# Attention on one core: TensorE's order written out, products with V in one run two tiles late, and half of a convolution's products on ScalarE

## The chip, the core and the metric

The kernel runs on one core of one Trainium2 chip. A core has five engines that run at the same time and wait for each other through semaphores: TensorE (PE in the profile; PEld is its weight loads), VectorE (DVE), ScalarE (ACT), GpSimd (POOL) and SyncE (SP), whose queue issues most DMAs. TensorE writes to PSUM, and the kernel divides the PSUM into banks of three groups: five called A, two called T, one called V. Everything else is in SBUF. The metric is the time of one execution on the device in microseconds (us); lower is better.

## The reference, cut to what matters

One step of a small diffusion transformer: two layers, 128 context tokens and 1024 latent tokens, 1024 channels, fp32. In each layer three mixers read the same normalised input, and their outputs are concatenated and projected:

```python
def layer(x, cond, lp, rope=None, ctx=None):
    mod = (silu(cond) @ lp['w_ada'] + lp['b_ada'])        # six vectors of 1024: shift, scale, gate, twice
    h = rmsnorm(x, lp['g_mix']) * (1 + sc1) + sh1
    comb = h @ lp['w_in']
    attn = mla_mixer(...)      # 8 heads; k is 64 + 32 rotary wide, v is 64 wide
    ssm = ssd_mixer(...)       # a state-space scan
    conv = conv_module(...)
    x = x + g1 * (concat([attn, ssm, conv]) @ lp['w_out'])
    ...                        # then a SwiGLU feed-forward, gated in the same way

def block_attention(q, k, v):  # for each block of 128 queries
    s = einsum('bqhd,bkhd->bhqk', qi, k) * scale
    p = softmax(s)
    return einsum('bhqk,bkhd->bqhd', p, v)

def conv_module(comb, lp):     # 256 channels
    g = comb[..., :256] * sigmoid(comb[..., 256:])
    g = dwconv(g, cm_conv_w, cm_conv_b)       # 31 taps along the tokens, per channel
    return silu(layernorm(g, cm_ln_g, cm_ln_b))
```

The context's queries see only the context's keys. The latent tokens' queries see 128 cached keys and the 1024 latent keys (1152).

## The kernel before, in words

**Layers and stages.** For each layer l the kernel projects the input (w_in), runs the scan, prepares the latents of attention, runs the attention loop, projects with w_out, and runs the feed-forward. The tokens are held as columns in three chunks of 384. Products that must keep fp32 accuracy are three matmuls on high and low parts (mm3, lines 103 to 105).

**The attention loop.** Eight heads are taken in four pairs i (prep_k and prep_q make a pair's keys and queries, prep_v and prep_r those of two pairs), and the 1152 queries in nine tiles t of 128 queries: 36 tiles in a layer. For one tile, `scores(j)` makes the scores of head j in three blocks of 384 keys (nine matmuls into three A banks), the maximum of each block on VectorE (line 805), their maximum and its negative (807, 808), and three exps on ScalarE (810), with the sums beside them. `attend` turns the probabilities: 18 transposes (831) of 128x128 into T banks, four at a time, copied to `pt` by VectorE (836) or ScalarE (84), and after each group of four the products with V (842) that belong to it, into the V bank. Two matmuls spread the reciprocal sums over the rows (853; ScalarE copies them to `rs`), and a product makes the output `mo` (856). Tile t = 0 is the context's, with one block of 128 keys. `attend` of a tile runs between the scores of the next one.

**Beside the tiles.** In layer 0 only, 80 steps of `adas` (186: eight small matmuls each, which make the modulation vectors of later stages) are drawn in between. In both layers `conv_taps` makes the convolution on GpSimd: for each half j of the 256 channels an initial product (869) and 30 taps, each a product into `ct` (872) and an addition into `acc` (78), over 1167 columns. A `copy` at 865 is its first instruction and holds it back to the start of the loop. `conv_norm` makes the layer norm of a chunk in four pieces: sums over channels on TensorE (882), centring (886), squares (890, 892, 78), sums of squares on TensorE (897), a reciprocal square root of ten small VectorE instructions (145 to 151), and a spread of it on TensorE (160), after which 905 and 906 finish.

**What sets the order.** The program is traced by a tile framework that inserts the semaphores and, by a simulated timeline, puts each engine's instructions into an order of its own: program order is a priority there, not the order on an engine. Each engine then executes its list in order. Pools with a fixed number of buffers (`bufs`) add waits: an exp's bank is free only when the exp has been read, a tile in SBUF only when its last reader is done. After the loop, line 971 loads the first w_out weights with load_w: ScalarE makes a high part `wh` (84), GpSimd the low part `wl` (81), 1024 columns each.

Of the kernel before, what the change touches and what calls it, by code (L numbers as in the profile page):

```python
# [8 lines left out]
F32 = mybir.dt.float32  # L9
# [8 lines left out]
KD = 8  # L18
# [35 lines left out]
def build(tc, nc, ap, dbg=None):  # L54
    V, S, G, PE, Q = nc.vector, nc.scalar, nc.gpsimd, nc.tensor, nc.sync
# [110 lines left out]
    def adas(rounds, stage=None, ahead=2):  # L166

        stage = stage or wp
        steps = [(l, r, q, k) for l, r in rounds for q in range(4) for k in range(0, KD, 2)]
        loads = []  # L170
        m = None
        for n in range(len(steps) + ahead):
            if n < len(steps):
                l, r, q, k = steps[n]
                loads.append(stage.tile([128, 1024], F32, tag="ws", name="ws", bufs=ahead + 1))
                Q.dma_start(loads[-1], ap["w_ada"][l, r, q, k // 2])
            if n >= ahead:
                l, r, q, k = steps[n - ahead]
                st = loads.pop(0)
                if k == 0:  # L180
                    m = sm.tile([128, 128], F32, tag="ms", name="ms", bufs=2)
                b = bank("A")
                for kk in range(2):
                    for j in range(4):
                        o = 512 * kk + 128 * j
                        PE.matmul(b[32 * j:32 * j + 32, :128], cond[:, k + kk, :], st[:, o:o + 128],
                                  start=kk == 0, stop=kk == 1)
                if k:
                    add_to(V, m, b[:, :128], m)
                else:  # L190
                    copy(m, b[:, :128])
                if k == KD - 2:
                    ada_end(l, r, q, m)
            yield
# [99 lines left out]
    first = adas([(0, 0)], sp, 6)  # L294
# [15 lines left out]
    for l in range(L):  # L310
# [397 lines left out]
        def prep_v(r, cs=range(NC3)):  # L708
            if r:
                vt[r] = hl_tile("vv", F32)[:, :2560].rearrange("p (t n) -> p t n", t=10)  # L710
            w = lat["w"][0]
            for c in cs:
                ck = lat[c][1]
                for t in range(KC[c][0] // 128, KC[c][1] // 128):
                    b0 = bank("A")
                    o = 128 * t - KC[c][0]
                    mm3(b0[:, :256], [(ck[:, 0, o:o + 128], ck[:, 1, o:o + 128],
                                       w[0][:, 512 + 256 * r:768 + 256 * r], w[1][:, 512 + 256 * r:768 + 256 * r])])
                    copy(vt[r][:, t], b0[:, :256])

        def prep_k(i, cs=range(NC3)):
            w = lat["w"][0]
            for c in cs:
                a, b = KC[c]
                b0 = bank("A")
# [18 lines left out]
        def prep_r(r, cs=range(NC3)):  # L744
            if r not in qr:
                qr[r] = at.tile([128, T], F32, tag="qr", name="qr", bufs=1)
            for c in cs:
                tb = [at.tile([128, CH], F32, tag="tb", name="tb", bufs=4) for _ in range(2)]
                for n in range(2):
                    Q.dma_start(tb[n], ap["rf"][:, c, n])  # L750
                    b0 = bank("A")
                    o = 512 * n + 128 * r
                    mm3(b0[:, :CH], [(wr[0][:, o + 256 * k:o + 256 * k + 128], wr[1][:, o + 256 * k:o + 256 * k + 128],
                                      lat[c][0][:, 0, k], lat[c][0][:, 1, k]) for k in range(2)])
                    V.tensor_mul(tb[n], tb[n], b0[:, :CH])
                add_to(V, qr[r][:, CH * c:CH * c + CH], tb[0], tb[1])
# [4 lines left out]
        prep_r(0, (0, 1))  # L761
        prep_k(0, (2,))
        prep_v(0, (2,))
        prep_r(0, (2,))
# [19 lines left out]
        class Tile_:  # L784


            def __init__(self, i, t, q, mo):
                self.i, self.t, self.q, self.mo = i, t, q, mo
                self.sl = small(8, "sl", 3)
                self.prs = []  # L790

            def scores(self, j):
# [3 lines left out]
                blocks = [(0, 128)] if t == 0 else [(128 + CH * b, CH) for b in range(3)]  # L796
                n = len(blocks)
                pr = at.tile([128, T], F32, tag="P", name="P", bufs=4)
                mx = small(4, "mx", 3)
                bs = []  # L800
                for b, (k0, w) in enumerate(blocks):
# [4 lines left out]
                if n > 1:  # L806
                    V.reduce_max(mx[:, 3:4], mx[:, 0:3], axis=AX.X)
                V.tensor_scalar_mul(mx[:, 3:4], mx[:, 3:4] if n > 1 else mx[:, 0:1], -SCALE)  # L808
                for b, (k0, w) in enumerate(blocks):
                    S.activation(pr[:, CH * b:CH * b + w], bs[b][:, :w], AF.Exp, bias=mx[:, 3:4], scale=SCALE,  # L810
                                 accum_out=sl[:, 3 * j + b:3 * j + b + 1])
                self.prs.append(pr)
                if j == 1:
# [4 lines left out]
                    else:  # L818
                        V.reciprocal(sl[:, 6:8], lv[:, :, 0])

            def attend(self):
                i, t, prs, sl, mo = self.i, self.t, self.prs, self.sl, self.mo
                vv = vt[i // 2]
                kts = [0] if t == 0 else list(range(1, 10))
                ob = bank("V")
                for a in range(0, len(kts), 2):
                    grp = kts[a:a + 2]
                    tb = bank("T")
                    for u in range(len(grp)):
                        for j in range(2):  # L830
                            PE.transpose(tb[:, 256 * u + 128 * j:256 * u + 128 * j + 128],  # L831
                                         prs[j][:, 128 * (a + u):128 * (a + u) + 128], ident)
                    pt = at.tile([128, 512], F32, tag="pt", name="pt", bufs=3)
                    w = 256 * len(grp)
                    if a % 4:
                        V.tensor_copy(pt[:, :w], tb[:, :w])  # L836
                    else:
                        copy(pt[:, :w], tb[:, :w])
                    for u, kt in enumerate(grp):
                        for j in range(2):  # L840
                            h = 2 * (i % 2) + j
                            PE.matmul(ob[64 * j:64 * j + 64, :128], vv[:, kt, 64 * h:64 * h + 64],  # L842
                                      pt[:, 256 * u + 128 * j:256 * u + 128 * j + 128],
                                      start=kt == kts[0], stop=kt == kts[-1])
                    if a == 4:
                        yield

                dl = at.tile([128, 2, 128], F32, tag="dl", name="dl", bufs=2)
                V.tensor_tensor(dl, ident.unsqueeze(1).to_broadcast([128, 2, 128]),
                                sl[:, 6:8].unsqueeze(2).to_broadcast([128, 2, 128]), ALU.mult)  # L850
                rb = bank("T")
# [3 lines left out]
                copy(rs, rb[:, :128])  # L855
# [4 lines left out]
        acc = [None, None]  # L860

        def conv_taps():
# [3 lines left out]
            for j in range(2):  # L866
# [45 lines left out]
        prev = iter(())  # L912
        qs = {}
        for i in range(NPAIR):
            if i:
                prep_k(i)
            if i == 2:
                prep_r(1)
            qs[i, 0] = prep_q(i, 0)
            for c in range(NC3):  # L920
                mo = at.tile([128, CH], F32, tag="mo", name="mo", bufs=2)
                for t in range(3 * c, 3 * c + 3):
                    cur = Tile_(i, t, qs[i, c], mo)
                    cur.scores(0)
                    if i == 2 and t == 1:
                        prep_v(1)
                    next(ag, None)
                    next(prev, None)
                    cur.scores(1)
                    next(ag, None)  # L930
                    drain(prev)
                    prev = cur.attend()
                    if t == 3 * c and c + 1 < NC3:
                        qs[i, c + 1] = prep_q(i, c + 1)
                    if t % 2:
                        next(ag, None)
# [4 lines left out]
        drain(prev)  # L941
        drain(norms)
        at.release()
# [27 lines left out]
        wo = [load_w(ap["w_out"][l, m]) for m in range(4)]  # L971
# [210 lines left out]
```

## Time and profile before

| | us |
|---|---|
| median of three runs (lowest, highest) | 3270.39 (3269.64, 3280.65) |
| the profiled execution, and its span | 3282.06, 3280.3 |
| PE busy in the span | 3120.5 (95%) |
| VectorE, ScalarE, GpSimd busy | 1754.9, 1144.7, 1070.2 |
| mean granted clock of TensorE | 0.976 |
| attention loop of layer 0, from line 865 to the last `mo` | 310.8 to 730.0 |
| attention loop of layer 1, from line 865 to the last `mo` | 1938.2 to 2314.1 |

A matmul is pipelined, and its recorded end is a model: a matmul of 384 columns is recorded with 0.34 us, though the next one starts 0.17 us later, so PE is not at its peak where it reads as busy. The granted clock is 1.0 at TensorE's full rate (2.4 GHz) and 0.5 at its lower one (1.2 GHz). A ScalarE exp is recorded with 0.58 us, and the next one starts 0.56 us after it.

### The profile page before, as it was taken

The numbers are of one execution on the slowest core, as the hardware profiler recorded it, in microseconds if no ns is written. First come the engines' busy times: TensorE is split into PE (matmuls) and PEld (weight loads), VectorE is DVE, ScalarE is ACT, GpSimd is POOL, SyncE is SP. The second block draws the span as 40 slices with busy tenths as digits, with TensorE's granted clock in tenths as the row PEclk, the third lists the DMA queues.
The fourth block names the chain that finished last, engine by engine and source line by source line (L and its number), as shares of the span: only waits on it lengthen the run. The fifth ranks groups of instructions, "written<-read, shape, count | busy, mean of one in ns | idle before, by whom it ended". The sixth has DMA issues, their size and how long they took to land. (4 is left out here: it accounts for less than half of the span.)

```text
span 3280.3 us, 50736 instructions
## 1 busy us (share of the span) xinstructions
PE 3120.5 (95%) x20610; PEld 2899.1 (88%) x20610; DVE 1754.9 (53%) x3891; ACT 1144.7 (35%) x2677; POOL 1070.2 (33%) x601
## 2 busy tenths in 40 slices
PE   6997998999999999999999989987999999999997
PEld 5986767779999999999999867766999999999997
DVE  6768777663633333333386687765373333333335
ACT  4465544562411111111144656555341111111113
POOL 2302998012511211112142049871242121122112
PEclk9998999999999999999999989998999999999998
DMA  6112333342111111111121020000401111111111
GB/s 236 49 30 86 115 117 105 123 173 76 52 39 39 45 46 39 39 39 52 47 95 55 25 64 8 20 15 22 149 27 51 40 46 46 39 39 52 39 33 58
DMA packets 67004, 202.38 MB, mean 62 GB/s; under 512 B 7889, under 2 KB 25425, under 8 KB 65233
## 3 DMA queue, kind: packets, MB, share of 16 engines
q1 hardware_dynamic: 63456, 194.02, 17.9%
q10 hardware_dynamic: 3312, 5.11, 0.4%
q8 instruction: 162, 2.65, 0.3%
q14 instruction: 74, 0.60, 0.1%
HBM read 177.44 MB, written 21.66 MB: 61 GB/s over the span
## 5 line engine op out<-in xcount | busy, mean ns | idle before, releaser
L81 POOL TENSOR_TENSOR wl<-ws,wh 128x1024 fp32r<-128x1024 f32 x164 | 396.0, 2421 | 1629.3 <-ACT wh L84 1549.3
L103 PE MATMUL psA<-hh,wh 128*128 128x384 f32 x2496 | 836.5, 337 | 4.4 <-ACT hh L270 2.7
L104 PE MATMUL psA<-hl,wh 128*128 128x384 f32 x2496 | 837.7, 336 | 1.1 <-DVE hl L267 0.7
L105 PE MATMUL psA<-hh,wl 128*128 128x384 f32 x2496 | 837.3, 336 | 0.0
L103 PEld LDWEIGHTS psA<-hh,wh 128*128 128x128 f32 x2496 | 471.0, 189 | 8.1 <-ACT hh L270 3.7
L104 PEld LDWEIGHTS psA<-hl,wh 128*128 128x128 f32 x2496 | 471.1, 189 | 3.9 <-DVE hl L267 1.2
L105 PEld LDWEIGHTS psA<-hh,wl 128*128 128x128 f32 x2496 | 471.0, 189 | 0.6
L999 DVE TENSOR_TENSOR fs<-fs,psA 128x384 f32<-128x384 f32 x132 | 72.9, 553 | 666.3 <-PE psA L105 657.4
L78 POOL TENSOR_TENSOR acc<-ct,acc 128x1167 f32<-128x1167 f32 x120 | 325.9, 2716 | 9.9
L84 ACT ACTIVATE wh<-ws 128x1024 fp32r<-128x1024 f32 (+1 forms) x178 | 184.8, 1049 | 405.2 <-PE psA L104 197.9
L998 ACT ACTIVATE fs<-psA 128x384 f32<-128x384 f32 x132 | 63.9, 485 | 655.1 <-PE psA L105 655.1
L810 ACT ACTIVATE P<-psA,mx 128x384 f32<-128x384 f32 (+1 forms) x400 | 224.1, 571 | 126.2 <-DVE mx L808 88.2
L1052 DVE SCALAR_TENSOR_TENSOR x<-psT,mod,x 128x384 f32<-128x384 f32 (+1 forms) x320 | 157.7, 513 | 198.6 <-PE psT L105 198.6
L805 DVE TENSOR_REDUCE mx<-psA 128x1 f32<-128x384 f32 (+1 forms) x400 | 208.9, 539 | 77.5 <-PE psA L105 74.9
L1052 DVE SCALAR_TENSOR_TENSOR x<-psA,mod,x 128x384 f32<-128x384 f32 (+2 forms) x384 | 186.7, 512 | 53.4 <-PE psA L105 46.9
L1002 DVE TENSOR_TENSOR fl<-fs,fh 128x384 fp32r<-128x384 f32 x132 | 167.5, 1270 | 65.9 <-ACT fh L84 65.9
L842 PE MATMUL psV<-pt,vv 128*64 128x128 f32 x2336 | 195.2, 289 | 6.7 <-DVE pt L836 5.0
L831 PE MATMUL psT<-cst,P 128*128 128x128 f32 x1168 | 194.5, 288 | 3.0 <-ACT P L810 1.1
L104 PE MATMUL psA<-fl,wh 128*128 128x384 f32 x576 | 193.2, 336 | 0.0
L105 PE MATMUL psA<-fh,wl 128*128 128x384 f32 x576 | 193.2, 335 | 0.0
L103 PE MATMUL psA<-fh,wh 128*128 128x384 f32 x576 | 190.0, 337 | 2.7 <-DVE fs L999 2.7
L103 PE MATMUL psA<-K,q 128*128 128x384 f32 (+1 forms) x400 | 159.1, 398 | 28.7 <-ACT P L810 22.5
(265 smaller groups left out, 5865.3 us busy)
## 6 DMA issues: line engine op xcount, KB each, us to landing
ws<-w_ada SPq DMA_DIRECT2D x96, 512.0 KB, 3.3
ws<-w_gate SPq DMA_DIRECT2D x44, 512.0 KB, 3.7
ws<-w_up SPq DMA_DIRECT2D x44, 512.0 KB, 3.6
ws<-w_down SPq DMA_DIRECT2D x44, 512.0 KB, 3.6
x<-xT SPq DMA_DIRECT2D x6, 1536.0 KB, 7.6
ws<-w_fm SPq DMA_DIRECT2D x16, 512.0 KB, 3.4
ws<-w_out SPq DMA_DIRECT2D x16, 512.0 KB, 3.7
mf<-mixed SPq DMA_DIRECT2D x18, 384.0 KB, 5.6
```

The source lines that it names most:

```text
L78: eng.tensor_tensor(out, a, b, ALU.add)
L81: eng.tensor_tensor(out, x, hi.bitcast(F32), ALU.subtract)
L84: S.activation(out, x, AF.Copy)
L103: PE.matmul(out, sh, mh, start=i == 0, stop=False)
L104: PE.matmul(out, sh, ml, start=False, stop=False)
L105: PE.matmul(out, sl, mh, start=False, stop=i == n - 1)
L805: V.reduce_max(mx[:, b:b + 1], b0[:, :w], axis=AX.X)
L810: S.activation(pr[:, CH * b:CH * b + w], bs[b][:, :w], AF.Exp, bias=mx[:, 3:4], scale=SCALE, accum_out=sl[:, 3 * j + b:3 * j + b + 1])
L831: PE.transpose(tb[:, 256 * u + 128 * j:256 * u + 128 * j + 128], prs[j][:, 128 * (a + u):128 * (a + u) + 128], ident)
L842: PE.matmul(ob[64 * j:64 * j + 64, :128], vv[:, kt, 64 * h:64 * h + 64], pt[:, 256 * u + 128 * j:256 * u + 128 * j + 128], start=kt == kts ...
L1002: V.tensor_sub(fl[:, sl], sg, fh[:, sl].bitcast(F32))
L1052: V.scalar_tensor_tensor(X[c][:, m, a:b], b0[:, a:b], modT[l][:, 40 + m, s:s + 1], X[c][:, m, a:b], ALU.mult, ALU.add)
```

## The change

**TensorE's order.** A small class stands in for the tensor engine. While the attention loop is traced, each matmul and transpose is made to depend on the one before it (without a semaphore), so that TensorE's list is the order of the program. The loop is written in the order that TensorE is to have. For one tile: the three blocks of scores of head 0; all 18 products with V of the tile two back and the two matmuls that spread its sums; two or three `adas` steps in layer 0; the first eight transposes of the tile before; two blocks of scores of head 1; eight transposes; the third block; the last two transposes; and behind them the queries of a next chunk, pieces of prep_r, three taps and, from tile 30 on, two pieces of the norm. `pt` becomes one buffer for a whole tile, `P` has three buffers for four, `mo` three for two, the spread sums go to free columns of the V bank, and `dl` (the diagonal of the reciprocals) is made in `scores`.

**The convolution.** For the half j = 0 the taps are unchanged. For j = 1 ScalarE makes each tap's product in two halves of 583 and 584 columns (`S.activation` with Copy and the tap's weight as scale), and GpSimd only adds, also in halves. Both halves of the channels use one `ct`.

**Smaller edits.** The w_out weights are loaded behind the last tap (`issue_after`). prep_v copies two tiles of V at a time; prep_k and prep_r take their banks before their first matmul; `adas` orders its loads differently and makes the same matmuls.

```diff
-    V, S, G, PE, Q = nc.vector, nc.scalar, nc.gpsimd, nc.tensor, nc.sync
+    V, S, G, Q = nc.vector, nc.scalar, nc.gpsimd, nc.sync
+    pin = {"on": False, "last": None}
+    def pinned(i):
+        if pin["on"]:
+            if pin["last"] is not None:
+                tc.add_manual_dep(i.ins, pin["last"], mybir.DependencyInfo(
+                    mybir.DependencyClass.NoSync, mybir.DependencyReason.DATA), reason="pinned")
+            pin["last"] = i.ins.name
+        return i
...
+            def turn(self):
+                self.pt = at.tile([128, 2, T], F32, tag="pt", name="pt", bufs=1)
+                todo = [(j, u) for u in range(len(self.kts)) for j in range(2)]
...
+                    tb = bank("T")
+                    for n, (j, u) in enumerate(part):
+                        PE.transpose(tb[:, 128 * n:128 * n + 128], self.pr[j][:, 128 * u:128 * u + 128], ident)
...
             def attend(self):
-                    tb = bank("T")
...
+                for u, kt in enumerate(self.kts):
+                    for j in range(2):
+                        h = 2 * (i % 2) + j
+                        PE.matmul(ob[64 * j:64 * j + 64, :128], vv[:, kt, 64 * h:64 * h + 64],
+                                  self.pt[:, j, 128 * u:128 * u + 128], start=u == 0, stop=u == n - 1)
                 for j in range(2):
-                    PE.matmul(rb[64 * j:64 * j + 64, :128], ones[:, 0:64], dl[:, j], start=True, stop=True)
+                    PE.matmul(ob[64 * j:64 * j + 64, 256:384], ones[:, 0:64], self.dl[:, j], start=True, stop=True)
...
                 for t in range(1, 31):
-                    G.tensor_scalar(ct[:, :CO], glu[j][:, t:t + CO], P("cw", w0 + t), 1.0, ALU.mult, ALU.mult)
-                    add_to(G, acc[j][:, :CO], ct[:, :CO], acc[j][:, :CO])
+                    for a, b in ((0, CO // 2), (CO // 2, CO)) if j else ((0, CO),):
+                        if j:
+                            S.activation(ct[:, a:b], glu[j][:, t + a:t + b], AF.Copy, scale=P("cw", w0 + t))
+                        else:
+                            G.tensor_scalar(ct[:, a:b], glu[j][:, t + a:t + b], P("cw", w0 + t), 1.0, ALU.mult, ALU.mult)
+                        last_tap[0] = G.tensor_tensor(acc[j][:, a:b], ct[:, a:b], acc[j][:, a:b], ALU.add)
                     yield
...
                     cur = Tile_(i, t, qs[i, c], mo)
-                    cur.scores(0)
+                    s0, s1 = cur.scores(0), cur.scores(1)
+                    if t:
+                        drain(s0)
+                    if pend:
+                        pend.attend()
                     if i == 2 and t == 1:
                         prep_v(1)
-                    next(ag, None)
-                    next(prev, None)
-                    cur.scores(1)
-                    next(ag, None)
-                    drain(prev)
-                    prev = cur.attend()
+                    step(ag, 2 + (t % 4 == 1))
+                    step(turn, 2)
+                    drain(s0)
+                    step(s1, 2)
+                    step(turn, 2)
+                    drain(s1)
+                    drain(turn)
+                    pend, prev, turn = prev, cur, cur.turn()
...
-                    for _ in range(3):
-                        next(taps, None)
-                    if 9 * i + t >= 25:
-                        next(norms, None)
+                    step(taps, 3)
+                    if 9 * i + t >= 30:
+                        step(norms, 2)
...
-        wo = [load_w(ap["w_out"][l, m]) for m in range(4)]
+        with tc.issue_after(last_tap[0].ins):
+            wo = [load_w(ap["w_out"][l, m]) for m in range(4)]
```

What the change does to the engines' lists is shown at three places of layer 1; the tiles' names carry numbers where two of a kind differ.

TensorE before, in pair 0: most of one tile and the start of the next (K and q make scores, psT holds transposes, psV the products with V).

```order
L842 MATMUL psV<-pt,vv 64x128 x8
L831 MATMUL psT<-cst,P 128x128 x6
L103 MATMUL psA<-K_18407,q_18713 128x384
L104 MATMUL psA<-K_18407,q_18713 128x384
L105 MATMUL psA<-K_18407,q_18713 128x384
...
L842 MATMUL psV<-pt,vv 64x128 x4
L831 MATMUL psT<-cst,P 128x128 x2
L842 MATMUL psV<-pt,vv 64x128 x4
L853 MATMUL psT<-dl,ones 64x128 x2
L842 MATMUL psV<-pt,vv 64x128 x2
L831 MATMUL psT<-cst,P 128x128
```

And TensorE after, in the same pair, one whole tile; the wrapper's two lines, 70 and 74, now stand for every matmul and transpose of the loop.

```order
L70 MATMUL psA<-K_18284,q_18618 128x384 x9
L70 MATMUL psV<-pt,vv 64x128 x18
L70 MATMUL psV<-dl,ones 64x128 x2
L74 MATMUL psT<-cst,P 128x128 x8
L70 MATMUL psA<-K_18285,q_18623 128x384 x6
L74 MATMUL psT<-cst,P 128x128 x8
L70 MATMUL psA<-K_18285,q_18623 128x384 x3
L74 MATMUL psT<-cst,P 128x128 x2
```

The kinds of work no longer alternate in groups of one to eight: a tile is seven groups, the same ones in every tile.

ScalarE before, in pair 1, from the 77th to the 85th exp of the loop.

```order
L810 ACTIVATE P,sl<-psA,mx 128x384 x3
L84 ACTIVATE pt<-psT 128x512 x2
L810 ACTIVATE P,sl<-psA,mx 128x384 x3
L84 ACTIVATE pt<-psT 128x256
L84 ACTIVATE rs<-psT 128x128
L810 ACTIVATE P,sl<-psA,mx 128x384 x3
```

And ScalarE after, from the 77th exp on, where the first products of the convolution (ct) stand.

```order
L104 ACTIVATE rs<-psV 128x128
L104 ACTIVATE pt<-psT 128x2x2x128
L912 ACTIVATE ct<-glu_17227,par 128x583
L912 ACTIVATE ct<-glu_17227,par 128x584
L104 ACTIVATE pt<-psT 128x2x2x128
L104 ACTIVATE pt<-psT 128x2x128
L912 ACTIVATE ct<-glu_17227,par 128x583
L847 ACTIVATE P,sl<-psA,mx 128x384 x3
L912 ACTIVATE ct<-glu_17227,par 128x584
L912 ACTIVATE ct<-glu_17227,par 128x583
```

From here 60 products stand among the exps and copies of 7.5 tiles; the first of them stands ahead of the 80th exp in ScalarE's list.

GpSimd before, late in the taps of the half j = 1: a low part of the w_out weights stands between a tap's product and its addition.

```order
L872 TENSOR_SCALAR ct<-glu_17349,par 128x1167
L81 TENSOR_TENSOR wl<-ws,wh 128x1024
L78 TENSOR_TENSOR acc_19856<-ct,acc_19856 128x1167
L872 TENSOR_SCALAR ct<-glu_17349,par 128x1167
```

And GpSimd after, where the half j = 0 ends and the half j = 1 begins.

```order
L914 TENSOR_SCALAR ct<-glu_16798,par 128x1167
L915 TENSOR_TENSOR acc_18630<-ct,acc_18630 128x1167
L915 TENSOR_TENSOR acc_19678<-ct,acc_19678 128x583
L915 TENSOR_TENSOR acc_19678<-ct,acc_19678 128x584
```

GpSimd has no product left in the half j = 1, and the four `wl` stand behind the last tap.

## Rows read from the trace of the kernel before

**Rows 1.** Windows, each loop in three; us, busy (instructions) per engine, clock, DMA.

```profile
310.80:446.30 135.50, 122.72 (x1253) 92.02 (x1254) 104.88 (x236) 68.42 (x205) 129.78 (x67) 0.96 0.35 117
446.30:564.30 118.00, 109.22 (x1090) 84.16 (x1089) 86.58 (x192) 58.59 (x176) 112.91 (x57) 0.97 0.32 108
564.30:730.00 165.70, 161.69 (x1656) 122.49 (x1654) 111.49 (x331) 101.58 (x274) 11.47 (x5) 1.00 0.42 143
1938.20:2062.30 124.10, 114.48 (x950) 93.70 (x951) 96.23 (x239) 78.85 (x231) 118.89 (x61) 0.99 0.03 11
2062.30:2170.50 108.20, 99.14 (x795) 83.36 (x794) 78.18 (x180) 63.24 (x184) 91.43 (x46) 0.94 0.05 15
2170.50:2314.20 143.70, 116.66 (x954) 91.08 (x952) 86.68 (x248) 83.18 (x219) 41.70 (x21) 0.89 0.14 47
```

**Rows 2.** Timeline of ScalarE, four exps; start us, us, engine, line, tiles.

```profile
446.33 0.59 ACT L810 ACTIVATE P<-psA,mx 128x384 f32<-128x384 f32 x1
564.32 0.59 ACT L810 ACTIVATE P<-psA,mx 128x384 f32<-128x384 f32 x1
2062.32 0.58 ACT L810 ACTIVATE P<-psA,mx 128x384 f32<-128x384 f32 x1
2170.47 0.59 ACT L810 ACTIVATE P<-psA,mx 128x384 f32<-128x384 f32 x1
```

**Rows 3.** Waits of the weight loads, layer 0; us, times, longest us.

```profile
PEld psV L842 <- issue: 17.8, 80, 0.4
PEld psT L831 <- issue: 17.7, 100, 0.3
PEld psA L186 <- issue: 10.3, 51, 0.4
```

**Rows 4.** The same, layer 1.

```profile
PEld psV L842 <- issue: 16.2, 77, 0.4
PEld psT L831 <- issue: 15.5, 86, 0.3
```

**Rows 5.** GpSimd's groups by shape, layer 1's loop; count, busy us, mean ns, idle.

```profile
L78 POOL TENSOR_TENSOR acc<-ct,acc 128x1167 f32<-128x1167 f32 x60 | 162.6, 2711 | 4.9
L872 POOL TENSOR_SCALAR ct<-glu,par 128x1167 f32<-128x1167 f32 x60 | 79.2, 1320 | 5.7
L869 POOL TENSOR_SCALAR acc<-glu,par 128x1167 f32<-128x1167 f32 x2 | 2.9, 1478 | 0.0
```

**Rows 6.** Timeline of GpSimd, layer 1, a `wl` among the taps; idle in brackets.

```profile
2193.66 2.37 POOL L81 TENSOR_TENSOR wl<-ws,wh 128x1024 fp32r<-128x1024 f32 x1 [16.88 <-PE psA L105]
```

**Rows 7.** GpSimd's groups by shape, whole span: other lengths.

```profile
L447 POOL TENSOR_TENSOR of<-xst,wd 128x512 f32<-128x512 f32 x18 | 20.9, 1164 | 101.8 <-ACT xst L84 101.8
L81 POOL TENSOR_TENSOR wlw_zb<-ws,whw_zb 128x792 fp32r<-128x792 f32 x2 | 4.3, 2158 | 4.8 <-ACT whw_zb L84 4.8
```

**Rows 8.** ScalarE's groups by shape, whole span.

```profile
L779 ACT ACTIVATE q<-qr,cst 64x384 fp32r<-64x384 f32 x48 | 29.5, 614 | 14.0 <-DVE qr L78 7.1 <-PE psA L105 5.9
L84 ACT ACTIVATE mh<-mf 128x384 fp32r<-128x384 f32 x48 | 20.7, 510 | 3.0 <-DMA mf<-mixed 1.6 <-DVE mo L856 1.5
L84 ACT ACTIVATE wh<-ws 128x832 fp32r<-128x832 f32 x8 | 7.2, 894 | 10.7 <-PE psA L104 6.5 <-issue 4.2
```

**Rows 9.** Waits of TensorE's matmuls, layer 1's loop.

```profile
PE psA L882 <- POOL acc L78: 19.7, 1, 19.7
PE psA L103 <- ACT P L810: 17.0, 14, 3.1
PE psT L897 <- DVE lsq L78: 2.6, 1, 2.6
```

**Rows 10.** Window behind the longest of these waits, columns as in Rows 1.

```profile
2228.30:2240.10 11.80, 9.15 (x33) 6.53 (x34) 5.20 (x20) 3.48 (x6) 0.00 (x0) 0.50 0.01 1
```

**Rows 11.** Timeline of VectorE, the first norm of layer 1: ends of its chain.

```profile
2234.90 0.16 DVE L899 TENSOR_SCALAR nv<-psT 128x3 f32<-128x3 f32 x1 [1.60 <-PE psT L897]
2237.50 0.56 DVE L157 TENSOR_TENSOR dg<-cst,ry 128x384 f32<-128x384 f32 x1
```

More of the change, by code (lines that the diff above doesn't have):

```diff
@@ L164, in build, with adas @@
     KO = (0, 4, 1, 5, 2, 6, 3, 7)
-    def adas(rounds, stage=None, ahead=2):
-        stage = stage or wp
-        steps = [(l, r, q, k) for l, r in rounds for q in range(4) for k in range(0, KD, 2)]
+    def adas(rounds, stage=None, ahead=2, per=1):
+        steps = [(l, r, q, k) for l, r in rounds for q in range(4) for k in range(0, KD, 2 * per)]
         loads = []
         m = None
[L172 to L193, printed above, removed]
@@ new lines, in load @@
+        def load(l, r, q, k):
+            bufs = 3 if stage is None else ahead + 1
+            sts = [(stage or wp).tile([128, 1024], F32, tag="ws", name="ws", bufs=bufs) for _ in range(per)]
+            for i, st in enumerate(sts):
+                Q.dma_start(st, ap["w_ada"][l, r, q, k // 2 + i])
+            loads.append(sts)
+        for s in steps[:ahead]:
+            load(*s)
+            if stage is not None:
+                yield
+        for n, (l, r, q, k) in enumerate(steps):
+            if stage is not None and n + ahead < len(steps):
+                load(*steps[n + ahead])
+            sts = loads.pop(0)
+            if k == 0:
+                m = sm.tile([128, 128], F32, tag="ms", name="ms", bufs=2)
+            b = bank("A")
+            for kk in range(2 * per):
+                for j in range(4):
+                    o = 512 * (kk % 2) + 128 * j
+                    PE.matmul(b[32 * j:32 * j + 32, :128], cond[:, k + kk, :], sts[kk // 2][:, o:o + 128],
+                              start=kk == 0, stop=kk == 2 * per - 1)
+            if k:
+                add_to(V, m, b[:, :128], m)
+            else:
+                copy(m, b[:, :128])
+            if stage is None and n + ahead < len(steps):
+                load(*steps[n + ahead])
+            if k == KD - 2 * per:
+                ada_end(l, r, q, m)
@@ L293, in build @@
     sp = pool("sp")
-    first = adas([(0, 0)], sp, 6)
+    first = adas([(0, 0)], sp, 6, 1)
     for _ in range(4):
@@ L742, in build, with prep_r @@
         qr = {}
-        def prep_r(r, cs=range(NC3)):
+        def prep_r(r, c):
             if r not in qr:
                 qr[r] = at.tile([128, T], F32, tag="qr", name="qr", bufs=1)
[L747 to L756, printed above, removed]
+            tb = [at.tile([128, CH], F32, tag="tb", name="tb", bufs=4) for _ in range(2)]
+            for n, b0 in enumerate([bank("A") for _ in range(2)]):
+                Q.dma_start(tb[n], ap["rf"][:, c, n])
+                o = 512 * n + 128 * r
+                mm3(b0[:, :CH], [(wr[0][:, o + 256 * k:o + 256 * k + 128], wr[1][:, o + 256 * k:o + 256 * k + 128],
+                                  lat[c][0][:, 0, k], lat[c][0][:, 1, k]) for k in range(2)])
+                V.tensor_mul(tb[n], tb[n], b0[:, :CH])
+            add_to(V, qr[r][:, CH * c:CH * c + CH], tb[0], tb[1])
         drain(so)
@@ L760, in build @@
         at = pool("at")
-        prep_r(0, (0, 1))
+        prep_r(0, 0)
+        prep_r(0, 1)
         prep_k(0, (2,))
         prep_v(0, (2,))
-        prep_r(0, (2,))
+        prep_r(0, 2)
         def prep_q(i, c):
@@ L788, in __init__ @@
                 self.i, self.t, self.q, self.mo = i, t, q, mo
+                self.blocks = [(0, 128)] if t == 0 else [(128 + CH * b, CH) for b in range(3)]
+                self.kts = [0] if t == 0 else list(range(1, 10))
                 self.sl = small(8, "sl", 3)
-                self.prs = []
+                self.pr = []
             def scores(self, j):
@@ L821, in attend @@
             def attend(self):
-                i, t, prs, sl, mo = self.i, self.t, self.prs, self.sl, self.mo
+                i, t, mo = self.i, self.t, self.mo
                 vv = vt[i // 2]
-                kts = [0] if t == 0 else list(range(1, 10))
                 ob = bank("V")
-                for a in range(0, len(kts), 2):
-                    grp = kts[a:a + 2]
-                    tb = bank("T")
[L829 to L851, printed above, removed]
+                n = len(self.kts)
+                for u, kt in enumerate(self.kts):
[3 more added lines that the diff above has]
+                                  self.pt[:, j, 128 * u:128 * u + 128], start=u == 0, stop=u == n - 1)
@@ L911, in build @@
         norms = chain_(*(conv_norm(c) for c in range(NC3)))
-        prev = iter(())
+        pend, prev, turn = None, None, iter(())
         qs = {}
+        pin.update(on=True, last=None)
+        qs[0, 0] = prep_q(0, 0)
         for i in range(NPAIR):
```

88 lines of the change are left out of this document (59 added, 29 removed).

## The prediction

> **What bounds the kernel now.** I read the two attention loops only, since everything outside them keeps its instructions. First the windows [rows 1]: each loop is cut in three where the new list of ScalarE has its first and its last product of the convolution. Counted in the lists, these stand behind the 67th and the 120th of 200 exps in layer 0 and behind the 79th and the 135th in layer 1; the starts of these exps in the trace [rows 2] are the borders. I call the parts A, B and C. The reader is to see that PE is busy for 122.7 of 135.5 us, 109.2 of 118.0 and 161.7 of 165.7 in layer 0, and for 114.5 of 124.1, 99.1 of 108.2 and 116.7 of 143.7 in layer 1, while ScalarE is busy for about half of A and B. PE is the bound, apart from the last part of layer 1. GpSimd is nearly as full in A and B: the convolution occupies it without a break.
>
> Second the waits of the weight loads for "issue" [rows 3, 4]: PE loses time where the kind of its work changes. The three large ones add to 45.8 us in layer 0, the two of layer 1 to 31.7. In the trace I counted 552 changes of kind (scores and preparations, transposes, products with V, adas) in layer 0 (175, 142 and 235 in A, B and C) and 445 in layer 1 (159, 124, 162), so one costs 0.083 and 0.071 us.
>
> Third PE's own waits in layer 1 [rows 9]: 19.7 us for the last addition of the convolution, then 2.6 for a sum of squares, and behind them 11.8 us at a granted clock of 0.50 [rows 10], half of which, 5.9 us, is lost. The convolution is late there because two `wl` of w_out stand among its taps; the later waited 16.9 us with GpSimd idle [rows 6]. In all 28 us of layer 1's C come from this.
>
> **The change part by part.** *TensorE's order.* The new list changes kind about 7 times in a tile and 8 with adas. For C's 14.4 tiles that is 115 in layer 0 for 235 and 105 in layer 1 for 162: 120 x 0.083 = 10 us and 57 x 0.071 = 4 us saved. The same in A (77 and 59 fewer) brings PE's work from 122.7 to 116 us and from 114.5 to 110; in B (82 and 71 fewer) from 109.2 to 102 and from 99.1 to 94. The matmuls are the same ones. A fixed order also takes from PE the freedom to fill a wait: in two of three norms in each layer the three small sums of squares and the spread that needs their square root now stand side by side. VectorE's chain between them runs from 2234.90 to 2238.06, 3.2 us [rows 11]; before, transposes and products of another tile lay beside it. Two in each layer cost 6.4 us.
>
> *The half j = 0 and part A.* Its taps are unchanged on GpSimd: two initial products of 1.48 us and 30 x (1.320 + 2.711 + 0.18 of gaps) = 126.3, in all 129.3 us from line 865 on [rows 5]. There is one `ct`, so ScalarE's first product for j = 1 must wait for the last of these additions, and behind it in ScalarE's list stand the copies of `pt` and the 68th or 80th exp, which PE needs. PE would be there after 116 and 110 us. So A ends at 129.3 in both layers: 6 us less than 135.5, and 5 more than 124.1. PE is held for 13 and 19 us. A stall of 19.7 us was followed by 5.9 us lost to the clock [rows 9, 10]; it could be nothing to 5.9 each time, and I take 2.5, 5 in all.
>
> *The half j = 1 and part B.* A product on ScalarE of 583 or 584 columns isn't in the trace. The nearest row is the same operation, Copy with a pointer as scale, at 384 columns: 614 ns; copies without it took 510 ns at 384 columns and 894 at 832, so 0.857 ns a column [rows 8]. 614 + 200 x 0.857 = 785 ns; bounds are 614 below and 894 above. Sixty make 47 us, added to the 58.6 and 63.2 us that ScalarE is busy with in the same exps now [rows 1]: 106 and 110 us. GpSimd's halves, half of 2.711 and a gap of 0.09, are 1.45 us each (between 1.16 for 512 columns and 2.16 for 792 [rows 7]), 87 us in all: beside it. PE's 102 and 94 us are also below ScalarE's. With 4% of idle between ScalarE's waits I take 110 and 115 us: 8 less than 118.0, 7 more than 108.2.
>
> By the Trainium skill ("ScalarE: Activation LUTs", section "What ACT_TABLE_LOAD costs") an ACTIVATE takes 186 ns and 0.833 ns a column, 93 more for a pointer, and 93 less back to back: an estimate of 765 ns, or 672 where the products follow one another. The 384-column row, 614 where the page gives 599, agrees. By it the sum would be 2 to 13 us lower.
>
> *Part C.* Layer 0: 10 saved, 6.4 lost, -3. Layer 1: the convolution ends at 129.3 + 115 = 244 us after line 865, before the first norm asks, so 22.3 us of waits and 5.9 of clock go; 4 are saved and 6.4 lost: -26. What is late next there is PE itself.
>
> *Edits at no cost.* The w_out weights' four `wl` behind the last tap take about 10 us of an idle GpSimd, some 100 us before w_out needs them; had w_out to wait, it would cost at most these 10. V's copies by two tiles, the other buffers, and adas' loads lie beside PE. A bank waited for by head 1's third block would show as before under "ACT P" [rows 9], 17 us in layer 1; I leave that size as it is.
>
> *Sum.* Layer 0: -6 - 8 - 3 = -17. Layer 1: +5 + 7 - 26 = -14. Clock +5. In all -26 us. The profiled execution took 3282.06 us (span 3280.3), so 3256 on its basis; it lies 11.7 above the median, 3270.39, and the median would become **3244**.
>
> **The rivals.** *More is saved.* Products at 614 ns (-20 in both layers, GpSimd's 87 us then still below), no clock lost (-5) and the norms' chains hidden because ScalarE and the other engines run ahead (-13): -64, 3206. For it speaks that PE's work in A and B is well below the floors; against it that 200 more columns must cost something. Chance 0.20.
>
> *No change that can be told.* ScalarE's list alternates products that wait for GpSimd with exps that wait for PE. If each waits in turn and B has 15% of idle rather than 4%, B is 12 us longer in both layers: -2, 3268. For it: the sum rests on one stall removed, and each part of layer 1 before it becomes longer. Against it: GpSimd has over 20 us to spare in B. Chance 0.24.
>
> *Slower.* The place is B. ScalarE's list is in order; a product that is not ready holds the exps, PE runs dry and its clock falls, as behind the 19.7 us [rows 9, 10]. If PE has the clock at 0.5 for half of B, its 102 and 94 us become 153 and 141: +43 and +26 over what I took, in all +43, 3313. It decides from the point where more than about 36% of B is at 0.5: then the gain of 26 is gone and the loss is over 16. For it: ScalarE is full in B, and PE idles for 8 and 21 us there by my sum. Against it: in A of layer 0 PE had 12.8 us idle and kept a clock of 0.96 [rows 1]. Chance 0.14. The Trainium skill ("TensorE: Matmul & The Clock Gate", Part 1) calls ScalarE's queue strictly first in, first out; nothing in the trace of before speaks against it, and this rival is what that rule would do here at its worst.
>
> That the change does not do what it says is excluded by the lists: PE's order is the written one.
>
> **How the numbers follow.** The forecast has 0.42, with its own range of 3228 to 3262. 0.5% is 16.4 us, about what a measurement can tell from no change: faster is below 3254, slower above 3287. Of the forecast's 0.42 some 0.31 lie below 3254. With 0.20 of the first rival and a little of the second that gives 0.53 for faster; 0.11 and 0.19 make 0.30 for the same; 0.14 and the second rival's tail make 0.17 for slower. The range goes from the first rival, 3204, to 3290, and leaves out most of the slower rival and the far end of the first.
>
> **What would show it.** In the profile after: the first product of ScalarE starts 129 us after GpSimd's first copy in both layers, with PE idle before it; a product lasts 0.78 us and a half addition 1.45; from the first to the last product 110 and 115 us, with ScalarE over 90% busy; the convolution's wait of 19.7 us is gone, and two waits of some 3 us stand at the norms in each layer; waits for "issue" fall by a third. Wrong would be: products shorter than 0.65 us, PE not held at the end of A, or a clock near 0.5 in a long stretch of B.

## The result: 1.3% slower, and the profile after

The changed kernel took 3316.85 us (median of four, 3311.05 to 3324.22) where the kernel before took 3275.52 beside it: a ratio of 1.0128, 95% interval 1.0105 to 1.0151, +41 us. The forecast was 3244. The profiled execution took 3311.95 us, its span is 3310.2, 29.9 longer than before (one of the faster executions after, one of the slowest before). Of this the two loops explain more than all: from GpSimd's first copy (now line 903) to the last `mo` (894), layer 0 takes 437.3 us for 419.3 and layer 1 393.2 for 375.9, +35.3 together; the rest of the span is 5.4 shorter.

The windows of the kernel after, cut at the same exps as [rows 1], the 67th and 120th of layer 0 and the 79th and 135th of layer 1 (columns as there). In layer 0 the last product of ScalarE stands behind the 114th exp in the trace, not behind the 120th that I had counted, so I cut at the exps, to have the same ones in a part (in layer 1 its products span 56 exps, some ten tiles and not 7.5):

```profile
308.40:447.80 139.40, 110.14 (x1190) 94.35 (x1180) 96.24 (x229) 69.91 (x203) 122.70 (x63) 0.93 0.32 110
447.80:565.20 117.40, 103.85 (x1129) 89.49 (x1126) 78.37 (x200) 99.79 (x236) 87.51 (x60) 0.98 0.31 108
565.20:745.70 180.50, 149.17 (x1670) 127.21 (x1668) 110.76 (x330) 102.12 (x271) 9.43 (x4) 0.95 0.36 123
1951.60:2097.90 146.30, 114.34 (x934) 100.69 (x934) 107.13 (x235) 79.57 (x230) 123.50 (x63) 0.92 0.03 9
2097.90:2206.80 108.90, 93.51 (x800) 81.57 (x797) 76.78 (x180) 99.87 (x238) 84.86 (x59) 0.97 0.03 10
2206.80:2344.80 138.00, 117.83 (x967) 101.99 (x965) 86.18 (x251) 85.10 (x222) 12.21 (x6) 0.89 0.17 56
```

The reader is to see two things. Part B, where ScalarE makes the products, takes as long as before: 117.4 us for 118.0, and 108.9 for 108.2. And PE is busy for less time than before in five of the six parts and for 1 us more in the last (688.8 us in all for 723.9), but the loops are longer: PE is idle for 141.7 us where it was idle for 71.3. What was saved in work went into waits, and more.

The work that was saved shows in the waits of the weight loads for "issue", of layer 0 and then of layer 1:

```profile
PEld psA L70 <- issue: 12.0, 39, 2.3
PEld psV L70 <- issue: 9.0, 36, 0.4
PEld psT L74 <- issue: 4.8, 24, 0.2
...
PEld psV L70 <- issue: 9.0, 34, 0.4
PEld psT L74 <- issue: 6.2, 34, 0.3
PEld psA L70 <- issue: 5.5, 10, 2.9
```

These are 25.8 and 20.7 us, where the larger kinds alone were 45.8 and 31.7 [rows 3, 4]; the changes of kind that I count fell from 552 to 328 and from 445 to 260. The waits of the matmuls themselves, in the loop of layer 0 and then of layer 1:

```profile
PE psA L70 <- ACT P L847: 29.2, 22, 2.2
PE psT L74 <- DVE ms L98: 18.0, 20, 2.3
PE psA L70 <- DVE dg L177: 8.4, 2, 5.1
...
PE psA L70 <- ACT P L847: 34.4, 25, 2.7
PE psA L70 <- DVE dg L177: 6.7, 2, 3.4
PE psT L74 <- DVE pt L874: 6.4, 6, 2.7
PE psA L70 <- DVE K L767: 6.3, 4, 3.0
```

Before, the waits for exps (ACT P) were 7.2 us in layer 0,

```profile
PE psA L103 <- ACT P L810: 7.2, 8, 2.5
```

and 17.0 in layer 1, and the wait of 19.7 us for the convolution was the largest [rows 9]; that one is gone. Three others stand in its place. In the timeline of the kernel after, in layer 1, with VectorE's and ScalarE's rows between PE's:

```profile
1996.40 0.77 PE L70 MATMUL psA<-K,q 128*128 128x384 f32 x3
...
1997.01 0.38 PE L74 MATMUL psT<-cst,P 128*128 128x128 f32 x2
1997.15 1.29 PE L70 MATMUL psA<-K,q 128*128 128x384 f32 x6
...
1998.95 0.14 DVE L845 TENSOR_SCALAR mx<-mx 128x1 f32<-128x1 f32 x1
1999.13 0.58 ACT L847 ACTIVATE P<-psA,mx 128x384 f32<-128x384 f32 x1 [1.32 <-DVE mx L845]
...
1999.86 0.79 PE L70 MATMUL psA<-K,q 128*128 128x384 f32 x3 [1.42 <-ACT P L847]
...
2284.48 0.56 DVE L177 TENSOR_TENSOR dg<-cst,ry 128x384 f32<-128x384 f32 x1
...
2285.09 1.01 PE L70 MATMUL psA<-dg,ones 128*128 128x384 f32 x1 [3.36 <-DVE dg L177]
```

Two blocks of a tile's head 0 run at 1997.15; the third needs an A bank, five serve in turn, and the next one still holds the previous tile's first block of head 1, whose exp waits for the maximum of all three. From the end of that tile's last block, at 1997.17, to the release of the bank 2.7 us go by, and TensorE has 1.3 us of work between. So it stands for 1.42 us with the products with V ready behind the waiting block. I count this wait of the third block 13 times in each loop, 19.1 and 22.3 us of the 29.2 and 34.4; four more in each, in the second tile of a pair, add 5.7 and 6.4. At 2285.09 it is the norm's spread, directly behind its sums. The 20 waits for `ms` in layer 0 are of the same kind:

```profile
401.46 0.40 PE L70 MATMUL psA<-ws,cond 128*32 128x128 f32 x8
...
401.79 0.68 DVE L98 TENSOR_TENSOR ms<-psA,ms 128x128 f32<-128x128 f32 x2
...
402.52 0.33 PE L74 MATMUL psT<-cst,ms 128*128 128x128 f32 x1 [0.66 <-DVE ms L98]
```

Each fourth step of adas ends in a transpose of the sum that VectorE has just begun to add; eight transposes of P stand behind it.

Last, GpSimd's timeline at the border of A and B in layer 0:

```profile
433.84 2.66 POOL L915 TENSOR_TENSOR acc<-ct,acc 128x1167 f32<-128x1167 f32 x1
450.37 2.82 POOL L915 TENSOR_TENSOR acc<-ct,acc 128x583 f32<-128x583 f32 x2 [13.87 <-ACT ct L912]
```

GpSimd was done with the half j = 0 at 436.5, 128.1 us after its first copy, and then stood for 13.9 us (in layer 1 for 19.6): TensorE's slow tiles brought ScalarE to its first product late, at 449.52 and 2099.25, not the other way round.

### The profile page after: what moved, and what is told of

It reads as the page before. It is cut to its first block, busy times and chain, and to the rows that moved or that the text cites. A ratio compares the mean times of both kernels' runs of the same rounds, so it can differ in the third digit from the quotient of the medians.

```text
span 3310.2 us, 50698 instructions
## 1 busy us (share of the span) xinstructions
PE 3082.8 (93%) x20610; PEld 2925.1 (88%) x20610; DVE 1745.4 (53%) x3891; ACT 1227.2 (37%) x2779; POOL 1001.9 (30%) x601
## 4 chain that ended last, share of the span: by engine, by line
PE 75%; DVE 12%; ACT 7%; issue 2%; DMA 1%; POOL 1%; SPq 0%; ACTq 0%; DVEq 0%; POOLq 0%
PE psA L70 61%; PE psT L70 8%; PE psT L74 4%; ACT P L847 3%; PE psV L70 3%; DVE mx L841 2%; DVE q L814 1%; ACT ct L912 1%; DVE nu L299 1%; POOL acc L915 1%; DMA ws<-w_ada 1%; DVE dl L858 1%; DVE hl L297 1%; DVE na L98 1%; DVE hl L301 1%
## 5 line engine op out<-in xcount | busy, mean ns | idle before, releaser
L915 POOL TENSOR_TENSOR acc<-ct,acc 128x1167 f32<-128x1167 f32 (+2 forms) x180 | 337.2, 1890 | 79.6 <-ACT ct L912 74.1
L70 PE MATMUL psA<-K,q 128*128 128x384 f32 (+1 forms) x1200 | 282.3, 368 | 79.8 <-ACT P L847 61.5
L70 PEld LDWEIGHTS psA<-K,q 128*128 128x128 f32 x1200 | 213.4, 202 | 102.6 <-ACT P L847 76.0
L74 PE MATMUL psT<-cst,P 128*128 128x128 f32 x1168 | 177.1, 288 | 18.4 <-DVE pt L874 10.6
```

Of the source, the lines that this page charges most:

```text
L70: return pinned(nc.tensor.matmul(*a, **k))
L74: return pinned(nc.tensor.transpose(*a, **k))
L915: last_tap[0] = G.tensor_tensor(acc[j][:, a:b], ct[:, a:b], acc[j][:, a:b], ALU.add)
```

## The experiments

Theory 1: the loss is in the chain. A matmul whose operand or bank isn't ready holds all matmuls behind it, where the old list had other work in that place. Theory 2, the rival: the loss is ScalarE's, whose products hold exps back. Ratios are to the kernel before, with 95% intervals.

**The chain alone taken out** (the rest of the change stays):

```diff
-        pin.update(on=True, last=None)
+        pin.update(on=False, last=None)
```

> The changed program with its new text, but TensorE's matmuls are not chained in the loop: the framework may order them by its own timeline. Theory 1 (the fixed order puts matmuls directly behind what they wait for; TensorE's waits in the two loops, about 137 us against 68 before, are the loss): most of these waits go and it comes near the kernel before or below it, 3245 to 3285 us. Theory 2 (ScalarE's products hold exps back in ScalarE's list and TensorE waits for them): the products are still there, so it stays above 3300.

Measured: 3242.66 us, 0.9904 (0.9888 to 0.9921). Its loops take 405.9 and 353.0 us:

```profile
309.20:715.10 405.90, 377.75 (x3979) 303.40 (x3971) 294.14 (x758) 268.94 (x706) 220.88 (x127) 0.97 0.36 124
1922.20:2275.20 353.00, 327.81 (x2695) 268.37 (x2695) 254.61 (x666) 263.04 (x685) 220.56 (x127) 0.98 0.08 29
```

PE is idle for 53.3 us. Its changes of kind are back at 495 and 457, and it is faster than before all the same. The chain costs 2.2%, about 73 us; theory 2 falls, since the products are still there.

**The products alone taken out, and alone put in.** In the changed kernel all taps go back to GpSimd; in the kernel before ScalarE makes the products of j = 1, with the w_out loads behind the last tap (the lines of the change's diff for both). The first edit:

```diff
-                    for a, b in ((0, CO // 2), (CO // 2, CO)) if j else ((0, CO),):
...
+                    G.tensor_scalar(ct[:, :CO], glu[j][:, t:t + CO], P("cw", w0 + t), 1.0, ALU.mult, ALU.mult)
+                    last_tap[0] = G.tensor_tensor(acc[j][:, :CO], ct[:, :CO], acc[j][:, :CO], ALU.add)
```

> The changed kernel, but all 60 taps' products are GpSimd's again, the order of TensorE stays fixed. Theory 1: the waits for the bank of the third block and for the small transposes stay; only the part in which ScalarE was over 90% busy gets shorter, by 0 to 20 us over both layers: 3297 to 3320. Theory 2: the loss goes with the products, 3270 to 3285.

Measured: 3336.77 us, 1.0194 (1.0178 to 1.0209). It lies 20 us above the changed kernel, so both theories had the sign wrong: theory 1 had it at the same time or faster, theory 2 faster. Theory 2 falls here too. PE is idle for 163.9 us in its loops, where the changed kernel has 141.7.

> The kernel before with only the convolution's change (ScalarE makes the products of the half j = 1 in two pieces, w_out's loads behind the last tap). Theory 1: TensorE's order is free, the wait of 19.7 us for the convolution in layer 1 goes, nothing else is lost: 3245 to 3275. Theory 2: slower than before by as much as the changed kernel, 3300 to 3320.

Measured: 3249.59 us, 0.9927 (0.9913 to 0.9942), as theory 1 said. With the fixed order the products on ScalarE are worth 0.7%. In the old text 0.7% is the worth of the products and the later w_out loads together.

**The third block.** It is moved behind the products with V, still in a fixed order:

```diff
                     if t:
-                        drain(s0)
+                        step(s0, 2)
                     if pend:
                         pend.attend()
+                    if t:
+                        drain(s0)
```

> The changed kernel, but the third block of head 0's scores stands behind the products with V (2.6 us later on TensorE) instead of ahead of them. Theory 1: the wait of 1.4 us for its bank, 26 times in both layers, 41 us, is covered by the products with V: 3275 to 3290. Theory 2: no change beyond 10 us, 3307 to 3320.

Measured: 3292.49 us, 1.0056 (1.0041 to 1.0071): 24 us off, of some 41 of waits. The matmuls' waits in its loop of layer 1:

```profile
PE psA L70 <- ACT P L847: 13.0, 14, 3.3
PE psT L74 <- ACT pt L104: 9.3, 14, 2.0
PE psT L74 <- DVE pt L874: 8.7, 15, 2.3
```

The waits for exps fell from 34.4 to 13.0 us, and those of the transposes for the copies of `pt` rose from 11.8 (5.4 and 6.4) to 18.0. The time is between the two theories' ranges, nearer to theory 1, and short of its size because a part of the waits moved on.

**Two more places.** adas' last transpose is put off until two blocks of head 1's scores are behind it; the norm runs one piece in a tile.

```diff
             if k == KD - 2 * per:
-                ada_end(l, r, q, m)
+                if stage is None:
+                    ends.append((l, r, q, m))
+                else:
+                    ada_end(l, r, q, m)
...
                     step(s1, 2)
+                    flush()
```

> The changed kernel, but the transpose that ends each fourth adas step (20 in layer 0) is put off until two blocks of head 1's scores are behind the step on TensorE's fixed list. The theory (waits of matmuls put directly behind what they need): its 20 waits of 0.9 us, 18 us, are covered, 12 to 20 us less: 3297 to 3305. A rival, that TensorE is late anyway and these waits only move on: 3312 to 3320.

Measured: 3304.69 us, 1.0098 (1.0081 to 1.0116).

```diff
-                    if 9 * i + t >= 30:
-                        step(norms, 2)
+                    if 9 * i + t >= 25:
+                        step(norms, 1)
```

> The changed kernel, but the norm of the convolution runs one piece in a tile from tile 25 on instead of two from tile 30 on, so that a tile's work stands between the sums of squares and the spread. The theory: two waits in each layer, 8.4 and 6.7 us, are covered: 3300 to 3308. The rival: they move on, 3312 to 3320. If the convolution isn't done at tile 25, a wait for it would show.

Measured: 3305.57 us, 1.0100 (1.0085 to 1.0116). Both times are in the range of their theory. But the first one's trace doesn't show the saving where it was expected: in layer 0 the loop takes 438.0 us for 437.3, and its waits are

```profile
PE psA L70 <- ACT P L856: 35.7, 24, 3.4
PE psA L70 <- DVE dg L177: 8.4, 2, 5.1
PE psA L70 <- DVE ms L98: 5.5, 2, 3.1
```

The 18.0 us for `ms` at the transposes are gone, and the waits for exps are 6.5 us longer. It is the loop of layer 1 that is shorter, 384.4 us for 393.2, where the edit leaves TensorE's list as it was; only ScalarE's and VectorE's differ in places. The range was met, but not where the theory's mechanism works. So I timed the changed kernel again.

> The changed kernel as it is, timed once more, because its four times so far lie 13 us apart and the two small moves (adas' transpose, the norm by pieces) are each worth no more than that. If the moves are real savings of 11 to 12 us, it is at 3314 to 3320 again; if it comes out at 3303 to 3308, they saved nothing and their waits only moved on.

Measured: 3315.44 us, 1.0134 (1.0115 to 1.0153). The two moves stand some 0.3% below it, with intervals that just touch these and overlap those of its first timing. That they save something is likely; where, one trace of each does not show.

**All three moves, in a fixed and in a free order.**

The three edits above together:

> The changed kernel with the three moves together: third block behind the products with V (which took 24 us off), adas' transpose put off, norm one piece at a time. The theory: the sum of the three, 24 + 16 + 12, so 3258 to 3275, still above the same program with a free order (3243), since waits for the copies of pt, for the queries and for P stay. The rival: one wait takes the other's place, 3280 to 3295.

Measured: 3280.69 us, 1.0022 (1.0012 to 1.0031): 36 us off the changed kernel, where the three alone add to 48, and half of what the chain costs. It missed the theory's 3258 to 3275. Its loops are 413.0 and 379.4 us; in layer 1 PE now waits 6.7 us for the convolution, since the norm begins at tile 25 there.

The edits of the third block and of adas, with the chain off:

> The changed program with TensorE's order free and two of the moves in its text (the third block behind the products with V, adas' transpose put off). The theory says that the moves repair what only a fixed order does: with a free order they change little, 3236 to 3250, against 3243 without them. A rival, that they are better places whatever sets the order: 3215 to 3232.

Measured, with the first two moves: 3238.26 us, 0.9902 (0.9885 to 0.9919), no difference from the free order without them that can be told. The move of the norm was not tried there. This and the free order itself are the fastest versions, and beat both kernels.

**What in the chain costs.** Only `attend`'s matmuls are chained to each other:

```diff
+                pin.update(on=True, last=None)
                 for u, kt in enumerate(self.kts):
...
                     PE.matmul(ob[64 * j:64 * j + 64, 256:384], ones[:, 0:64], self.dl[:, j], start=True, stop=True)
+                pin["on"] = False
```

> The changed program with only the 18 products with V and the two sums' matmuls of a tile chained to each other; all else on TensorE may be ordered by the framework. If the loss is in the chain over the different kinds of work (the theory), this stays within 10 us of the free order: 3235 to 3253. If the run of products with V is what delays the scores, it goes up by 20 us or more: above 3262.

Measured: 3242.10 us, 0.9915 (0.9900 to 0.9929), the free order's time. By instruction, tiles and shapes TensorE, VectorE, ScalarE and GpSimd execute the same lists here as in the free order, with the same 495 and 457 changes of kind. Such a chain doesn't keep other work out from between the products, and it moved nothing that the trace shows. So this is a second timing of the free order, and decides nothing between the theory and its rival; what an unbroken run of products alone would cost stays open.

And the chain with the old text, with nothing else changed (the class as in the change's diff):

```diff
+        pin.update(on=True, last=None)
         for i in range(NPAIR):
```

> The kernel before with only the chain: TensorE executes the loop in the order of the old text, which was written as a priority and not as an order. The theory: every product with V stands directly behind the copy that it needs and every exp's bank is waited for, so the loss is larger than in the changed kernel, over 3350. A rival, that the chain itself costs nothing and the rewritten places do: 3265 to 3285.

Measured: 3708.84 us, 1.1340 (1.1296 to 1.1384). Its waits in the first 490 us of layer 0's loop, which takes 608.8:

```profile
PE psV L70 <- ACT pt L104: 62.0, 78, 3.6
PE psV L70 <- DVE pt L856: 43.7, 49, 2.5
```

In that text each group of products with V follows the transposes and the copy that feed it, and all of TensorE waits for every copy. Set beside the changed kernel, the rewriting has taken most of that away: the two-tiles-late products have no such wait left. The same chain costs 13.4% in the old text and 2.2% in the new one.

**The rewritten text alone**, with the first two edits of this section, a free order and all taps on GpSimd:

> The changed program with TensorE's order free, as in the first experiment, and all products of the convolution on GpSimd, as in the second. It leaves the rewritten loop and the smaller edits alone. If ScalarE's products are worth the same 20 to 24 us as with the fixed order and in the old loop, 3260 to 3270. If the free order gains from the rewriting alone, 3243 to 3250; if the rewriting is worth nothing, it is at the kernel before, 3270 to 3276.

Measured: 3254.21 us, 0.9945 (0.9930 to 0.9960), between the cases that I had named. So the rewriting with the smaller edits saves about 18 us, the products on ScalarE another 13 on top of it, and the chain costs 73. The rewritten loop and the smaller edits were not separated. In this trace PE doesn't wait for the convolution either, though all its products are GpSimd's: the last tap ends 256 us after the first copy, and the norm asks later. So the later w_out loads and the later norm are enough to end the wait of 19.7 us, without the products.

## Why the prediction was wrong

**The step that failed** is "PE would be there after 116 and 110 us". I took PE's busy time, subtracted the saved changes of kind, and set the time to the end of A to that, as if TensorE would not wait. PE was busy for 110.1 and 114.3 us there, so the work was nearly right; the part took 139.4 and 146.3 us, for 29.3 and 32.0 of idle time, where my sum ends it at 129.3. The same omission is in part C: 180.5 and 138.0 us where my sum has 162.7 and 117.7. In layer 1 the convolution's wait did go from C, as forecast, and C is still only 5.7 us shorter. The sentence that let it pass is the one on the edits at no cost: a bank waited for "would show as before", "I leave that size as it is". The waits for exps went from 24 to 64 us in the two loops. It was the third block of head 0, not of head 1. The new list has the place: the bank is held for the maxima, small steps of VectorE and an exp, 2.7 us in the trace, and only two transposes and two blocks, 1.3 us, stand ahead of the third one. Without the chain the two loops are 72 us shorter, with PE idle for 53.3 us in place of 141.7.

I wrote that a fixed order takes from PE the freedom to fill a wait, and then applied it to the norms alone. There it held: 6.4 us in each layer forecast, 8.4 and 6.7 measured. The same sentence holds for each place where a matmul stands behind one whose result it needs through another engine. adas' transposes, 18.0 us of waits, I did not list at all; when they were put off, the loop of layer 0 became no shorter, so not every wait on such a list is a loss of its own size.

**What held.** The changes of kind fell to 260 in layer 1, where my shares add to 258, but only to 328 in layer 0, for 273; their waits fell by more than the third that I had named. A product on ScalarE takes 787 ns, forecast 785; a half addition 1.48 us, forecast 1.45. By the Trainium skill ("ScalarE: Activation LUTs", section "What ACT_TABLE_LOAD costs") two in a row would be 765 + 672 = 1.437 us, an estimate; the trace has 1.44 for the two at 449.52. The rows of the two engines:

```profile
449.52 1.44 ACT L912 ACTIVATE ct<-glu,par 128x583 f32<-128x583 f32 x2
```

```profile
L912 ACT ACTIVATE ct<-glu,par 128x584 f32<-128x584 f32 x60 | 47.3, 788 | 2.8 <-POOL acc L915 2.4
L912 ACT ACTIVATE ct<-glu,par 128x583 f32<-128x583 f32 x60 | 47.2, 786 | 1.8 <-POOL acc L915 1.3
...
L915 POOL TENSOR_TENSOR acc<-ct,acc 128x583 f32<-128x583 f32 x60 | 88.9, 1481 | 57.6 <-ACT ct L912 57.5
```

B took 117.4 and 108.9 us for 110 and 115, near in the sum and not in the parts. The convolution's wait of 19.7 us went. GpSimd's half j = 0 ended after 128.1 us for 129.3, but the hold that I derived from it did not occur, for the reason above, and its absence was one of my signs of being wrong; ScalarE waited 3.7 us for GpSimd in all.

**The rivals.** The slower one has the sign, but its mechanism is wrong. It put the loss in B, with ScalarE's products holding exps; B is as long as before, its clock was 0.98 and 0.97, and without the products the kernel is slower still. The loss lies in A of both layers and C of layer 0 (3.9, 22.2 and 14.8 us longer), where ScalarE is busy for little more than half the time. The rival of no change is wrong in the same place: it has ScalarE's products and exps wait in turn in B, and ScalarE waited 3.7 us for GpSimd in all. No rival had TensorE wait by its own fixed list.

The clock has a share. In A it was 0.93 and 0.92 for 0.96 and 0.99 [rows 1], means between the levels of 1.2 and 2.4 GHz, with no stall as long as the 19.7 us of before but many of 1 to 3 us; in the free order it was 0.97 and 0.98 over the loops. A stretch at a mean clock of 0.93 loses at most 7% of its time to it. Summed in this way over the rows, that is 51 us in the loops of the changed kernel and 19 in those of the free order. So, as an estimate, some 30 of the 73 us may be the clock's; the exact shares of clock and waits were not separated.

## What to carry to other kernels

To fix an engine's order is to promise that each instruction will be ready when its turn comes: go along the new list and write beside each entry what it waits for, through which engine, and what work stands between. A place with some 1.5 us too little, 13 times in each of two loops, cost 41 us of waits, and TensorE's busy time fell by 35 us in all. Where a scheduler can choose, first give it the better program text and the emptier engine: here these gave 1.0% without any chain. Three moves repair half of the fixed order's loss, and two of them did nothing that can be told for the free one.

## What was not expected of the hardware

Two of VectorE's instructions, with all their operands in SBUF, are up to five and seven times as long beside GpSimd's work. In the timeline of the kernel after:

```profile
2002.22 2.73 POOL L915 TENSOR_TENSOR acc<-ct,acc 128x1167 f32<-128x1167 f32 x1
2002.44 2.93 DVE L814 SCALAR_TENSOR_TENSOR q<-qr,cst,q 64x384 fp32r<-64x384 f32 x1
```

Away from GpSimd's work the same instruction takes 0.62 us, and `dl` (858) 0.42 with up to 2.93 beside it; subtractions with an operand in PSUM, such as line 809, stay at 0.55. The kernel before has the same, up to 2.92 and 2.82 us. In a fixed order such a delay reaches TensorE: the transposes at 2006.35 waited 0.85 us for a copy of `pt` that stood behind this instruction on VectorE.

By the Trainium skill ("GPSIMD Engine Reference", section "1. Specifications") GpSimd shares its SBUF interfaces with VectorE and contends with VectorE's instructions of two SBUF inputs; the trace agrees, with the numbers above, and shows no such delay for instructions with one input in PSUM.
